# A two-layer hybrid attention backbone on one core: additions behind the value batches, neighbouring queries for the maxes, and a longer lead

## The chip, the cores and the metric

The kernel runs on one core of one Trainium2 chip. It is one program with one launch; its time is the device time of that launch in microseconds, and the median of several runs counts. The engines are named as the profile names them: PE (TensorE, matmuls), PEld (TensorE's weight loads, which run beside matmuls), DVE (VectorE), ACT (ScalarE), POOL (GpSimd) and SP (SyncE, which issues every DMA of this kernel, in program order).

## The reference

Two layers work on 2048 latent tokens and 256 context tokens of width 1024. In each layer the tokens are normalised and projected once; three mixers share the projection: an attention with low-rank queries and keys (six heads, here MLA), a grouped-query attention (six heads that share two key heads, here GQA), and a convolution. Their outputs are gated, concatenated and projected back. What the change touches is the softmax of the two attentions:

```python
def one_block(qi):
    s = jnp.einsum('bqgrd,bkgd->bgrqk', qi, k).astype(jnp.float32) * scale
    p = jax.nn.softmax(s, axis=-1).astype(v.dtype)
    return jnp.einsum('bgrqk,bkgv->bqgrv', p, v)
...
o_mla = block_attention(q_mla, jnp.concatenate([k_mla, k_mla_c], axis=1),
                        jnp.concatenate([v_mla, v_mla_c], axis=1))
...
y = jnp.concatenate([o_mla, o_gqa, o_conv], axis=-1) * jax.nn.silu(p[..., OFF_GATE:])
x_new = x + gate[:, None, :] * (y @ w_out)
```

All data are float32. Latent queries look at all 2304 keys. The first layer also computes the context tokens' own attention (256 queries, 256 keys); the last layer doesn't.

## The kernel before

The program alternates projections and attention: the projection of layer 0, the attention of layer 0, a stage that holds layer 0's output projection and layer 1's input projection, the attention of layer 1, and the last output projection. The change lies in `attention` (line 1369) and, in one place, in `first_unit` (line 1249), which belongs to the projections.

**Units and steps.** The attention of a layer runs through `units`: one for each head and each chunk of queries. The GQA heads (numbers 6 to 11) come first, then the MLA heads (0 to 5). A chunk has 512 queries; layer 0 has a fifth chunk with the 256 context queries. A unit has 9 steps (`j` from 0 to 8), each for a pair of 128-key tiles; the unit of the context chunk has one. The order of all the instructions is written out by the loop at line 1604: what one turn of it issues is one step.

**Scores.** `s_pair` (line 1478) issues the score matmuls of a step: two key tiles run side by side in the upper and lower 64 rows of the array, with 4 such pairs of matmuls for a GQA head and 5 for an MLA head. Values are split in a high and a low part, so there are several products. The last product (`qd`) adds the negated maximum of each query, which stands as a row of 512 numbers in partitions 32 and 96 of the tile `qd`. ACT then takes the exponential into a tile `p` of 128 x 1024, from a ring of 8 buffers (`buffer`, line 1388).

**Maxes.** The maximum of each query must be known before its unit starts. `max_stream` (line 1434) computes it ahead, from the high parts alone: for each of 4 groups of 128 queries it multiplies queries by keys into PSUM tiles `m` (three banks, `p_m`), and DVE reduces each bank to a column of `mx`. A generator turn issues one pair of banks of 512 keys (8 turns) or, in the ninth turn, all four groups with the last 128 keys, and then the final reduction into `nm`, 128 partitions x 4. Here the queries are the stationary operand: group q takes every fourth query, `x[r, q:512:4]`, so partition p of column q belongs to query 4p + q, and the four numbers of a partition are neighbours in the row. Each step of the loop takes one turn of this stream, and the first four steps two (`behind = LEAD - 9`), so that the stream stays `LEAD` = 13 turns ahead of the steps. The stream also loads the queries of the next unit when it starts a unit (`load_q`, line 1413; 4 DMAs for a GQA unit and 10 for an MLA unit, five sets of query buffers).

**Rows.** `rows_step` (line 1421) moves the maxes from `nm` to the row of `qd` through DRAM: one step after `nm` it issues the store, and two steps later the two loads into the partitions 32 and 96.

**Value batches.** `pv_pair` (line 1536) multiplies a tile `p` with the values into the PSUM tile `o`. These are not issued at once: the loop collects steps in `pend` and issues them as batches, 5 pairs at `j` = 5 and the last 4 at `j` = 0 of the next unit (line 1620; batches of 3 in the last head). With the last pair of a unit, ACT copies `o` to `e`, and two DMAs store it.

**Sums.** `sums` (line 1499) adds up the tiles `p` of a unit on POOL, one 128 x 1024 addition a step, into `acc`. In GQA units the last two tiles are first added on DVE (`d`), at `j` = 8, and POOL adds `d`. Three steps after the unit's last, at `j` = 2 of the next, `fold_step` (line 1524) adds the two halves of `acc` on DVE into `f`. `finish` (line 1557) sums `f` over the partitions with a matmul by ones, for two units at a time, at the head of a value batch.

**Beside it**, while the heads 0 to 5 run, a planner (`out_proj.sch.poll()`) mixes in tasks of the next output projection (`y_k`, line 622): they divide the attention's outputs by the sums and multiply with the gates, on DVE and ACT, in tiles `lent` and `big`.

Of the kernel before, what the change touches and what calls it, by code (L numbers as in the profile page):

```python
# [9 lines left out]
F32 = mybir.dt.float32  # L10
# [277 lines left out]
def hybrid_dit(ctx: ExitStack, tc: tile.TileContext, I: dict, out: bass.AP):  # L288
# [163 lines left out]
    def projections(l):  # L452
# [796 lines left out]
        def first_unit():  # L1249
# [16 lines left out]
            def lane():  # L1266
                while todo:
                    n, e, q = todo.pop(0)
                    o, w = n * 512, min(512, NK - n * 512)
                    ps = (yield from aux.take())[:, 0:w]  # L1270
                    r = slice(64 * e, 64 * e + 64)
                    T.matmul(out=ps, lhsT=a[r, q:512:4], rhs=kH[0][r, o:o + w], start=True, stop=True)
                    yield ps
                    V.tensor_reduce(out=mx[:, q, 2 * n + e:2 * n + e + 1], in_=ps, op=ALU.max, axis=AX.X)
                    aux.give(ps)
                    left[0] -= 1
                    yield
# [6 lines left out]
            row = z.nm[u]  # L1284
            save(row.rearrange("(p j) -> p j", p=128), nm, nt)
            yield lambda: INF if clk.pending[key(row)] else 0.0
# [82 lines left out]
    def attention(l, out_proj):  # L1369
        z = scratch[l]  # L1370
        with ExitStack() as ps_:
# [49 lines left out]
            def rows_step():  # L1421
                for r in rows_due:
                    r[0] -= 1
                    h, c = u = r[1]
                    row = z.nm[h, c]
                    if r[0] == ROW_OUT:
                        dma(row.rearrange("(p j) -> p j", p=128), r[2].bitcast(F32))
                    elif r[0] == 0:
                        for o, i in m_parts(u, qt[u], row):
                            dma(out=o, in_=i)  # L1430
                while rows_due and rows_due[0][0] <= 0:
                    rows_due.pop(0)

            def max_stream():
                for i, u in enumerate(units[1:], 1):
                    h, c = u
                    n = CH[c][1] // 128
                    if 1 < i + 1 < len(units):
                        load_q(units[i + 1])
                    a, _, cr, _ = qt[u]  # L1440
# [8 lines left out]
                    def scores(ps, q, o, w, at=0):  # L1449
                        for i, (x, y) in enumerate(ops):  # L1450
                            for e in range(2):
                                r = slice(64 * e, 64 * e + 64)
                                T.matmul(out=ps[e][:, at:at + w], lhsT=x[r, q:CH[c][1]:n], rhs=y[r, o:o + w],
                                         start=(i == 0), stop=(i == len(ops) - 1))
# [13 lines left out]
                    for e in range(2):  # L1468
# [3 lines left out]
                                    negate=True)  # L1472
                    rows_due.append([ROW_OUT + 1, u, nm[:, 0:n]])
                    yield
# [24 lines left out]
            def sums(u, j, p, N):  # L1499

                s = st.setdefault(u, {})
                side = u[0] >= MH and N > 2
                if j == 0:
                    s["acc"] = p
                    if N == 1:
                        folds.append([3, u])
                elif j == 1:
                    acc = ac.tile([128, 1024], F32, tag="acc", name="acc")
                    add(G, acc, s["acc"], p)
                    s["acc"] = acc  # L1510
                elif side and j == N - 2:
                    s["p"] = p
                elif side and j == N - 1:
                    d = buffer(u)
                    add(V, d, s.pop("p"), p)
                    add(G, s["acc"], s["acc"], d)
                else:
                    add(G, s["acc"], s["acc"], p)
                if j == N - 1 > 0:
                    folds.append([3, u])  # L1520

            folds = []

            def fold_step(now=False):

                for f in folds:
                    f[0] -= 1
                while folds and (now or folds[0][0] <= 0):
                    u = folds.pop(0)[1]
                    W = CH[u[1]][1]  # L1530
# [5 lines left out]
            def pv_pair(u, j, t, N, p):  # L1536
# [6 lines left out]
                for e in range(2):  # L1543
                    T.matmul(out=s["o"][e * 64:e * 64 + 64, :], lhsT=v[:, t + e, :], rhs=p[:, e * W:(e + 1) * W],
                             start=(j == 0), stop=(j == N - 1))
                if j == N - 1:
                    e1 = op.tile([128, 512], F32, tag="e1", name="e1")[:, 0:W]
                    A.activation(out=e1, in_=s["o"], func=AF.Copy)
# [5 lines left out]

            fin = []

# [23 lines left out]
            LAG = 1  # L1580
            ROW_OUT = 2
            LEAD = 13
            qt[units[0]], qt[units[1]] = qall[0:2]
# [20 lines left out]
            for u, j, t, N in steps:  # L1604
# [9 lines left out]
                if behind:  # L1614
                    behind -= 1
                    next(stream)
                fold_step()
                sums(u, j, p, N)
                pend.append((u, j, t, N, p))
                if len(pend) >= LAG + batch(pend):  # L1620
                    finish()
                    for x in [pend.pop(0) for _ in range(batch(pend))]:
                        pv_pair(*x)
                out_proj.sch.poll()
                h, c = u
# [3 lines left out]
            while pend:  # L1629
                finish()  # L1630
                for x in [pend.pop(0) for _ in range(batch(pend))]:
                    pv_pair(*x)
            fold_step(True)
            finish(True)
# [92 lines left out]
```

## Time and profile before

| what | value |
|---|---|
| median of 3 runs | 4333.98 us (4333.17 to 4342.68) |
| the profiled execution | 4335.15 us, of which 4333.4 us are its span |
| mean granted TensorE clock | 0.962 |
| attention of layer 0, GQA heads, then MLA heads | about 787 to 1386 us, then to 2075 us |
| attention of layer 1, GQA heads, then MLA heads | about 2930 to 3496 us, then to 4129 us |

The page of the profile gives each engine's busy time, and the share of the span that it is. The view of stretches gives the same for chosen stretches of time, with the clock that TensorE was granted (1.00 is full speed; it takes the values 1.0 and 0.5, so a mean of 0.93 says that 14% of the stretch ran at half speed). The view of waits tells for which engine's work an engine stood idle. In the rows of instructions a time in square brackets is the idle time of the engine just before, and what ended it. Nearly all instructions go through one helper and stand under one line, L159, so that the tiles tell them apart: `s` and `qd` are scores, `m` and `mx` maxes, `nm` the negated maxes, `f` the folds, `o` the value products, `e` their copies.

### The profile page before, as it was taken

Reading aid. Unit: us, or ns where it says so; the run is one execution under the profiler, and the core shown is the slowest. Engines: PE = TensorE matmul, PEld = TensorE weight load, DVE = VectorE, ACT = ScalarE, POOL = GpSimd, SP = SyncE. Lnnn points to the kernel's source line nnn. Section 1 sums busy time; section 2 is a strip of 40 time slices with the busy share of each in tenths; the row PEclk is TensorE's granted clock in tenths of the full one; section 3 lists DMA queues with packets and bytes.
Section 4 is the critical chain, followed back from the end, with each engine's and each line's share of the span. In section 5 each row is a group of like instructions: output and inputs, shape, how many; then the busy total and the mean of one; then the engine's idle time right before and its main releaser. Section 6 shows DMA issues by size and latency. Waiting matters only on the chain. (4 is left out here: it accounts for less than half of the span.)

```text
span 4333.4 us, 60999 instructions
## 1 busy us (share of the span) xinstructions
PE 4082.3 (94%) x22542; PEld 2834.6 (65%) x22542; DVE 2449.4 (57%) x3771; ACT 1891.8 (44%) x2503; POOL 2482.6 (57%) x1277
## 2 busy tenths in 40 slices
PE   7999899999999999999879998999999999999988
PEld 4778467665555666665668787776556566666566
DVE  4643378555655645456533554886555574555663
ACT  4553356444443333333334544664444444433342
POOL 2541263576766776666434423537777777777744
PEclk8999999999999999999989999999999999999999
DMA  5555454411313332233854453543121143232384
GB/s 184 158 163 166 155 163 156 93 39 36 60 39 71 96 74 56 66 67 103 244 184 154 139 174 122 172 145 68 35 57 38 43 103 69 66 77 62 102 260 146
DMA packets 384213, 477.13 MB, mean 110 GB/s; under 512 B 128190, under 2 KB 200583, under 8 KB 383915
## 3 DMA queue, kind: packets, MB, share of 16 engines
q1 hardware_dynamic: 383914, 473.24, 38.7%
q8 instruction: 177, 2.90, 0.3%
q14 instruction: 122, 0.99, 0.1%
HBM read 329.79 MB, written 134.85 MB: 107 GB/s over the span
## 5 line engine op out<-in xcount | busy, mean ns | idle before, releaser
L159 DVE TENSOR_REDUCE mx<-m 128x1 f32<-128x512 f32 (+2 forms) x1716 | 1084.5, 680 | 1020.8 <-PE m L159 1012.6
L159 PE MATMUL mm<-big,wh 128*128 128x512 f32 (+2 forms) x4240 | 1300.8, 390 | 74.0 <-DVE big L159 30.6
L159 POOL TENSOR_TENSOR acc<-acc,p 128x1024 f32<-128x1024 f32 x482 | 1183.6, 2456 | 279.6 <-ACT p L159 202.2
L159 ACT ACTIVATE p<-s 128x1024 f32<-128x1024 f32 (+1 forms) x682 | 695.2, 1020 | 874.7 <-PE s L159 789.1
L159 PEld LDWEIGHTS mm<-big,wh 128*128 128x128 f32 (+1 forms) x4240 | 776.1, 189 | 311.6 <-issue 77.2
L159 PE MATMUL s<-qh,big 64*128 64x512 f32 (+1 forms) x3504 | 829.9, 411 | 0.2
L159 PE MATMUL mm<-big,wl 128*128 128x512 f32 (+2 forms) x2120 | 808.7, 381 | 3.6 <-POOL wl L159 3.6
L159 POOL TENSOR_TENSOR wl<-wraw,wh 128x1024 fp32r<-128x1024 f32 (+2 forms) x148 | 314.4, 2130 | 740.7 <-ACT wh L159 688.1
L159 PE MATMUL o<-p,big 128*64 128x512 f32 (+1 forms) x2728 | 689.0, 622 | 0.7 <-ACT e L159 0.7
L159 PE MATMUL m<-big,qh 64*128 64x512 f32 (+1 forms) x2304 | 587.4, 412 | 96.8 <-DVE mx L159 96.6
L159 PEld LDWEIGHTS m<-big,qh 64*128 64x128 f32 x2304 | 491.6, 309 | 156.9 <-DVE mx L159 130.1
L159 PEld LDWEIGHTS s<-qh,big 64*128 64x128 f32 x3504 | 434.1, 189 | 197.3 <-issue 165.4
L159 PEld LDWEIGHTS mm<-big,wl 128*128 128x128 f32 (+1 forms) x2120 | 401.2, 189 | 83.3 <-POOL wl L159 4.9
L159 PEld LDWEIGHTS o<-p,big 128*64 128x64 f32 x2728 | 201.6, 144 | 377.8 <-issue 370.9
L159 PE MATMUL s<-ql,big 64*128 64x512 f32 (+1 forms) x1752 | 421.5, 393 | 0.0
L159 POOL TENSOR_TENSOR acc<-acc,wraw 128x1024 f32<-128x1024 f32 x142 | 344.4, 2426 | 81.8 <-ACT wraw L159 45.0
L159 DVE SCALAR_TENSOR_TENSOR aux<-wn,par,aux 128x512 f32<-128x512 f32 (+1 forms) x396 | 259.1, 720 | 121.8 <-ACT aux L159 121.4
L159 ACT ACTIVATE wraw<-s 128x1024 f32<-128x1024 f32 (+1 forms) x194 | 198.3, 1022 | 242.3 <-PE s L159 197.4
L159 POOL TENSOR_TENSOR sb<-sb,sb 128x512 f32<-128x512 f32 (+1 forms) x161 | 194.5, 1216 | 156.7 <-ACT sb L159 127.3
L159 PE MATMUL m<-big 64*128 64x512 f32 (+1 forms) x1032 | 261.8, 406 | 1.3 <-DMA big<-qm 1.2
L159 PE MATMUL s<-qd,zm 33*128 33x512 f32 (+1 forms) x876 | 234.7, 406 | 6.3 <-DMA qd<-nm 6.3
L159 POOL TENSOR_TENSOR acc<-p,p 128x1024 f32<-128x1024 f32 x52 | 124.8, 2399 | 199.4 <-ACT p L159 199.4
(168 smaller groups left out, 4772.1 us busy)
## 6 DMA issues: line engine op xcount, KB each, us to landing
wraw<-in_w_in SPq DMA_DIRECT2D x80, 512.0 KB
o<-e SPq DMA_DIRECT2D x192, 128.0 KB
big<-o SPq DMA_DIRECT2D x96, 256.0 KB
wraw<-in_w_out SPq DMA_DIRECT2D x48, 512.0 KB
sb<-in_w_mod SPq DMA_DIRECT2D x77, 256.0 KB
sb<-in_x SPq DMA_DIRECT2D x61, 256.0 KB
big<-kn SPq DMA_DIRECT2D x48, 288.0 KB
sb<-x SPq DMA_DIRECT2D x54, 256.0 KB
```

Source lines behind the costliest of these rows:

```text
L159: return f(**kw)
```

## The change

Five things change; the result computed is the same.

1. The fold and the DVE half of the sums move. The addition of the last two tiles `p` is issued by `pv_pair` with the unit's last value pair, behind the matmuls of that batch. The fold of a unit is issued behind the first batch after that whose head belongs to a unit of 9 steps. In the order of DVE's instructions the addition moves from `j` = 8 to `j` = 0 of the next unit, and the fold from `j` = 2 of the next unit to `j` = 5, in both cases behind the maxes of that step and with a value batch on PE.
2. A group of the maxes takes 128 neighbouring queries. Partition p of column q now belongs to query 128q + p, so the store of the row writes single numbers (512 pieces of 4 bytes instead of 128 of 16).
3. The two loads of a row come three steps after its store instead of two.
4. `LEAD` is 16 instead of 13: the first seven steps take two turns of the stream.
5. When the stream starts the fourth chunk of a head, it loads the queries of two units instead of one.

```diff
@@ first_unit
-                    T.matmul(out=ps, lhsT=a[r, q:512:4], rhs=kH[0][r, o:o + w], start=True, stop=True)
+                    T.matmul(out=ps, lhsT=a[r, q * 128:q * 128 + 128], rhs=kH[0][r, o:o + w], start=True, stop=True)
...
-            save(row.rearrange("(p j) -> p j", p=128), nm, nt)
+            save(row.rearrange("(j p) -> p j", p=128), nm, nt)
@@ rows_step
-                    if r[0] == ROW_OUT:
-                        dma(row.rearrange("(p j) -> p j", p=128), r[2].bitcast(F32))
+                    if r[0] == ROW_IN:
+                        dma(row.rearrange("(j p) -> p j", p=128), r[2].bitcast(F32))
                     elif r[0] == 0:
                         for o, i in m_parts(u, qt[u], row):
                             dma(out=o, in_=i)
...
+            loaded = [1]
+
             def max_stream():
                 for i, u in enumerate(units[1:], 1):
                     h, c = u
                     n = CH[c][1] // 128
-                    if 1 < i + 1 < len(units):
-                        load_q(units[i + 1])
+                    ahead = i + 2 if c == 3 else i + 1
+                    while loaded[0] < min(ahead, len(units) - 1):
+                        loaded[0] += 1
+                        load_q(units[loaded[0]])
...
-                                T.matmul(out=ps[e][:, at:at + w], lhsT=x[r, q:CH[c][1]:n], rhs=y[r, o:o + w],
+                                T.matmul(out=ps[e][:, at:at + w], lhsT=x[r, q * 128:q * 128 + 128], rhs=y[r, o:o + w],
...
-                    rows_due.append([ROW_OUT + 1, u, nm[:, 0:n]])
+                    rows_due.append([ROW_IN + 1, u, nm[:, 0:n]])
@@ sums
                 if j == 0:
                     s["acc"] = p
-                    if N == 1:
-                        folds.append([3, u])
...
                 elif side and j == N - 1:
-                    d = buffer(u)
-                    add(V, d, s.pop("p"), p)
-                    add(G, s["acc"], s["acc"], d)
+                    s["last"] = s.pop("p"), p, buffer(u)
                 else:
                     add(G, s["acc"], s["acc"], p)
-                if j == N - 1 > 0:
-                    folds.append([3, u])
...
-            def fold_step(now=False):
-
-                for f in folds:
-                    f[0] -= 1
-                while folds and (now or folds[0][0] <= 0):
-                    u = folds.pop(0)[1]
+            def fold_step():
+
+                while folds:
+                    u = folds.pop(0)
@@ pv_pair
                 if j == N - 1:
+                    if "last" in s:
+                        p0, p1, d = s.pop("last")
+                        add(V, d, p0, p1)
+                        add(G, s["acc"], s["acc"], d)
+                    ended.append(u)
@@ the loop
             LAG = 1
-            ROW_OUT = 2
-            LEAD = 13
+            ROW_IN = 3
+            LEAD = 16
...
-                fold_step()
                 sums(u, j, p, N)
                 pend.append((u, j, t, N, p))
                 if len(pend) >= LAG + batch(pend):
                     finish()
+                    if pend[0][3] > 1:
+                        folds += ended
+                        ended.clear()
                     for x in [pend.pop(0) for _ in range(batch(pend))]:
                         pv_pair(*x)
+                    fold_step()
...
-            fold_step(True)
+            folds += ended
+            fold_step()
             finish(True)
```

More of the change, by code (lines that the diff above doesn't have):

```diff
@@ L1553, in pv_pair @@
                     fin.append(u)
-            fin = []
+            fin, ended = [], []
             def finish(last=False):
```

## The prediction

> **What bounds the kernel now.** First the busy times of the page, then the view of stretches for the four parts of the two attentions (start and end, length, busy time of PE, PEld, DVE, ACT and POOL, granted clock):
>
> ```profile
> span 4333.4 us, 60999 instructions
> PE 4082.3 (94%) x22542; PEld 2834.6 (65%) x22542; DVE 2449.4 (57%) x3771; ACT 1891.8 (44%) x2503; POOL 2482.6 (57%) x1277
> ```
> ```profile
> 816.00:1360.00 544.00, 507.48 (x3050) 315.25 (x3052) 322.81 (x508) 228.43 (x247) 372.81 (x155) 0.93 0.20 44
> 1360.00:2070.00 710.00, 668.40 (x4466) 444.56 (x4464) 398.37 (x575) 269.37 (x297) 490.39 (x200) 0.98 0.33 77
> 2958.00:3472.00 514.00, 488.01 (x2960) 300.66 (x2958) 305.36 (x483) 222.72 (x232) 372.48 (x154) 0.94 0.18 42
> 3472.00:4122.00 650.00, 634.29 (x4306) 424.63 (x4306) 376.10 (x543) 261.10 (x277) 490.83 (x200) 0.99 0.33 80
> ```
>
> PE is the bound everywhere; a gain must come out of its idle time, its lost clock or its own work. In the GQA parts (first and third row) it idles 36.5 of 544 us and 26 of 514, and the clock is 0.93 and 0.94. The waits say for whom (total, times, longest): the rows `qd` in the whole run, then the maxes in the first and in the second GQA part.
>
> ```profile
> PE s L159 <- DMA qd<-nm: 22.7, 10, 3.4
> ```
> ```profile
> PE m L159 <- DVE mx L159: 32.7, 27, 2.2
> ```
> ```profile
> PE m L159 <- DVE mx L159: 23.4, 22, 1.1
> ```
>
> What DVE does at such a wait stands in the timeline of one GQA unit, DVE first, then PE:
>
> ```profile
> 962.02 1.50 DVE L159 TENSOR_TENSOR f<-acc 128x512 f32<-128x512 f32 x1
> 963.45 2.47 DVE L159 TENSOR_REDUCE mx<-m 128x1 f32<-128x512 f32 x4
> 966.34 1.29 DVE L159 TENSOR_REDUCE mx<-m 128x4 f32<-128x512 f32 x2 [0.42 <-PE m L159]
> 972.37 3.68 DVE L159 TENSOR_REDUCE mx<-m 128x1 f32<-128x512 f32 x6 [4.52 <-PE m L159]
> 975.96 1.22 DVE L159 TENSOR_TENSOR p<-p,wraw 128x1024 f32<-128x1024 f32 x1
> ```
> ```profile
> 962.76 0.39 PE L159 MATMUL m<-big,qh 64*128 64x512 f32 x1
> 964.18 0.62 PE L159 MATMUL m<-big,qh 64*128 64x512 f32 x1 [1.03 <-DVE mx L159]
> ```
>
> Two maxes a step take DVE about 1.2 us (four in 2.47), and a GQA step without a value batch is no longer than that. So the fold, 1.50 us between them, has no room: all three banks of `m` are full, and PE stands 1.03 us. Around the value batch the same DVE idles 4.52 us.
>
> The stall also costs clock. Four units of layer 1, two without and two with a lost window, then the 3.4 us that hold a stall and the 3.4 us behind them:
>
> ```profile
> 3240.00:3261.50 21.50, 20.42 (x134) 13.14 (x134) 13.93 (x23) 9.84 (x10) 16.99 (x7) 1.00 0.16 38
> 3331.10:3354.10 23.00, 21.93 (x134) 13.80 (x136) 13.86 (x21) 9.79 (x11) 16.93 (x7) 0.93 0.14 36
> 3308.70:3331.10 22.40, 21.33 (x138) 13.61 (x140) 13.92 (x23) 10.46 (x12) 16.97 (x7) 1.00 0.15 37
> 3354.10:3378.10 24.00, 22.93 (x138) 13.74 (x140) 13.97 (x23) 10.45 (x12) 16.92 (x7) 0.93 0.13 35
> ```
> ```profile
> 1013.40:1016.80 3.40, 2.34 (x20) 1.96 (x19) 2.98 (x4) 1.84 (x2) 3.32 (x2) 1.00 0.01 0
> 1016.80:1020.20 3.40, 3.40 (x13) 1.35 (x13) 2.27 (x5) 1.02 (x1) 3.24 (x3) 0.50 0.11 21
> ```
>
> Same work (x134 each, x138 each), 1.5 and 1.6 us longer at a mean of 0.93, which is 2 x 0.07 x 23 = 3.2 us at half clock. An us at half clock thus loses about 0.47 us.
>
> **The change part by part.** Everything is worked out against the profiled execution, 4335.15 us (span 4333.4); the median of the runs is 4333.98, 1.2 us less.
>
> *A, folds in the GQA parts.* Moved to `j` = 5, the fold starts after that step's maxes (DVE is through with those of 966.34 at 967.6) and has until the maxes of 972.37. The 4.5 us hold the 1.50 us, and also the two folds behind a context chunk (the longer one takes 2.65, below). The addition of 975.96 moves behind the maxes that follow it, into the same sort of gap at `j` = 0; POOL waits for it there as before, with a busy time of 17 us in a unit of 21.5. The stalls go: 32.7 + 23.4 = **56 us**. Late next is DVE itself, 2 x 0.6 us a step against PE's step, a few tenths in a unit, counted in E.
>
> *B, their clock.* 2 x 0.07 x 544 + 2 x 0.06 x 514 = 138 us at half clock, times 0.47: **65 us**. The rounding of the clock leaves 5 us either way.
>
> The page "TensorE: Matmul & The Clock Gate" of the Trainium skill (Part 1, The HAM clock gate) has the clock fall after a whole idle window of about 3.4 us. Here 1.06 us of idling (3.40 - 2.34) within a busy window was enough, so the trace doesn't bear it out; by the page B would be nothing, a rival below.
>
> *C, rows.* The loads of a row wait in SP's queue behind query loads: in the worst place, at the fourth chunk of an MLA head, ten DMAs of each of two units come between. A store and its loads in a GQA unit, and SP's waits for the landing of such a store:
>
> ```profile
> 3248.44 0.32 SPq L1366 DMA_DIRECT2D nm<-nm  x1
> ...
> 3251.29 0.68 SPq L1366 DMA_DIRECT2D qd<-nm  x2
> ```
> ```profile
> SPq L1366 <- DMA nm<-nm: 5.3, 5, 2.3
> ```
>
> Three more steps of lead, one of them spent before the loads, leave four steps instead of two between load and use: at least 2 x 1.2 = 2.4 us more, and at the fourth chunk ten of the twenty query loads are issued a unit earlier. The longest wait is 3.4 us. I take all of it, **23 us**. The MLA parts lose 2 x 0.02 x 710 + 2 x 0.01 x 650 = 41 us to half clock, 19 us by the same 0.47; of this I take half, **10 us**, for waits of this kind and of D, since other stalls stay.
> The store in 512 pieces isn't in the trace. From the issue of the store to its load 2.9 us pass now (3248.44, 3251.29), SP has waited for its landing 2.3 us at most. Between no change and four times that, 9 us, nothing comes late: seven steps and a value batch, some 13 us, lie between store and use. I take nothing.
>
> *D, folds behind the context chunk in MLA units of layer 0.* One of six such places, with both stalls, and the longer DVE fold of a GQA one:
>
> ```profile
> 1734.28 0.62 PE L159 MATMUL m<-big,qh 64*128 64x512 f32 x1 [1.32 <-DVE mx L159]
> ...
> 1736.80 0.45 PE L159 MATMUL m<-big,qh 64*128 64x128 f32 x1 [0.51 <-DVE mx L159]
> ```
> ```profile
> 984.27 2.65 DVE L159 TENSOR_TENSOR f<-acc 128x512 f32<-128x512 f32 x1
> ```
>
> 5 x 1.8, and 1.3 in the last head, which has the first stall alone: **10 us**. The stalls behind `lent` and `big` (the planner's tasks) stay.
>
> *E, neighbouring queries.* Weight loads of one form, strided in `m`, contiguous in `s`; then PE at the scores of a context unit, and from the start to the end of an MLA unit's ninth turn:
>
> ```profile
> L159 PEld LDWEIGHTS m<-big,qh 64*128 64x128 f32 x2304 | 491.6, 309 | 156.9 <-DVE mx L159 130.1 <-issue 0.4
> L159 PEld LDWEIGHTS s<-qh,big 64*128 64x128 f32 x3504 | 434.1, 189 | 197.3 <-issue 165.4 <-ACT p L159 3.2 <-ACT wh L159 0.8
> ```
> ```profile
> 974.54 0.28 PE L159 MATMUL s<-qh,big 64*128 64x256 f32 x1
> 974.66 0.28 PE L159 MATMUL s<-ql,big 64*128 64x256 f32 x1
> ```
> ```profile
> 3583.67 0.55 PE L159 MATMUL m<-big,qh 64*128 64x128 f32 x2
> ...
> 3585.47 0.45 PE L159 MATMUL s<-qh,big 64*128 64x512 f32 x1
> ```
>
> Under 512 columns the 309 ns are hidden by the matmul running. In the ninth turn the matmuls have 128 columns, and the load is the bound: 8 pairs in 1.80 us (3583.67 to 3585.47), 0.225 a pair. Contiguous loads kept up with 0.12 a pair (974.54, 974.66), so 8 x 0.105 = 0.84 us go in an MLA unit, 0.42 in a GQA unit, of which I take 0.3 because DVE's 1.2 us a step is late next. 48 x 0.84 + 46 x 0.3, and 3 us in the context units: **57 us**. Bounds: nothing, if the step of the queries isn't what makes the load long; 87 us, if a pair gets down to half of 0.12 us, as its columns are half of those at 974.54.
>
> The same page (section LDWEIGHTS) lets the time of a load hang on the number of columns alone. The 309 against 189 ns speak against that; by the page E would be nothing, the second rival.
>
> *F, the start of each attention.* Three more steps take two turns, and there DVE is the bound:
>
> ```profile
> 788.18 4.88 DVE L159 TENSOR_REDUCE mx<-m 128x1 f32<-128x512 f32 x8 [0.85 <-PE m L159]
> ```
>
> 2.44 us a step instead of 1.2: 3.7 us in a layer, with some half clock 4, so **8 us** more in two.
>
> ```profile
> 4107.87 19.35 POOL L159 TENSOR_TENSOR acc<-acc,p 128x1024 f32<-128x1024 f32 x7
> ```
>
> The steps at the end of an attention that have no maxes now gain nothing, since there POOL's additions, one behind the other to the end of the stage, set it.
>
> Sum: 56 + 65 + 23 + 10 + 10 + 57 - 8 = 213 us. 4334 - 213 = **4121 us**. The forecast's own range, from the rounding in B, half to all of C and D, and 35 to 75 us in E: 4080 to 4155.
>
> **The rivals.** *The clock stays*, because something else in each GQA unit halves it, such as the turn of 128-column matmuls: B and the 10 us are lost, 4121 + 75 = 4196 us. For it speaks that the lost window comes right behind that turn as well as behind the stall; against it, that MLA units with twice as long a turn run at 0.99. *The load stays long*, because of the operand and not its step: 4121 + 57 = 4178. Against it: the 2304 loads at 309 are all strided, the 3504 at 189 all contiguous. *The stall moves* on to `j` = 6 and 7, because the fold waits behind POOL in its new place for longer than the batch lasts: A and B are lost, 4121 + 121 = 4242. The 2.65 us of 984.27 are such a wait, and they fit in 4.52. *Slower*: the store of a row in 512 pieces takes so long that the scores wait for it at the first step of every unit. It decides from 13 us, 25 ns a piece if they go one by one; each us beyond costs 96 us in 96 units, so at 15.2 us everything is given back, and at 16 us it is 4121 + 288 = 4409. For it speaks only that no such store is in the trace; against it the 2.3 us that SP waited for one of 128 pieces.
>
> **How the numbers follow.** Forecast 0.66, load 0.10, clock 0.08, moved stall 0.06, slower 0.06; 0.04 is left for what I don't see, half of it within 0.2% of the time before, which is about what a measurement can tell from no change. Faster by more than 0.2%: 0.92; within: 0.02; slower: 0.06. The range holds the forecast's, the load's and the clock's cases: 4075 to 4197.
>
> **What would show it.** In the GQA parts the wait of `m` for `mx` near zero and the clock at 0.99 or more (A, B); folds under a value batch; no wait for `qd` (C); weight loads of `m` near 189 ns, the MLA turn near 1 us (E); more waits in the first unit (F). The forecast is wrong if GQA units without a stall still show windows at 0.5, if the loads of `m` stay at 309, or if SP stands at the store of the rows.

## The result, and the profile after

The changed kernel takes 4397.68 us (median of 4 runs, 4384.36 to 4405.24) against 4333.57 us before: 1.014 times the time, 95% interval 1.0108 to 1.0172. It is slower, by 64 us where 213 us less were forecast. The profiled execution took 4391.08 us. First the busy times of its page, then the view of stretches for the GQA and MLA parts of layer 0 and of layer 1:

```profile
span 4389.3 us, 61080 instructions
...
PE 4012.7 (91%) x22542; PEld 2670.0 (61%) x22542; DVE 2501.8 (57%) x3771; ACT 1892.2 (43%) x2504; POOL 2478.5 (56%) x1277
```
```profile
823.00:1345.00 522.00, 495.37 (x3214) 288.04 (x3216) 357.61 (x531) 238.15 (x257) 390.18 (x161) 0.97 0.33 48
1347.00:2071.00 724.00, 629.67 (x4281) 384.25 (x4282) 388.26 (x549) 259.23 (x287) 473.88 (x194) 0.92 0.37 74
2971.00:3476.00 505.00, 479.25 (x3126) 281.40 (x3126) 338.16 (x505) 232.58 (x242) 391.40 (x162) 0.97 0.28 45
3476.00:4177.00 701.00, 612.28 (x4134) 370.21 (x4133) 363.58 (x513) 250.07 (x265) 472.23 (x194) 0.92 0.34 71
```

The rows of the kernel before that the prediction shows hold other numbers of matmuls (3050 in the first, 3214 here). These stretches of the kernel before end with the same parts and hold about as many as the rows above:

```profile
814.00:1383.50 569.50, 532.66 (x3216) 331.34 (x3214) 337.43 (x533) 237.75 (x257) 391.78 (x162) 0.93 0.20 44
1384.00:2064.00 680.00, 639.45 (x4276) 426.47 (x4274) 378.58 (x550) 255.96 (x282) 467.58 (x191) 0.97 0.34 79
2951.00:3489.50 538.50, 512.16 (x3123) 317.14 (x3121) 320.07 (x508) 233.96 (x243) 390.68 (x162) 0.95 0.18 42
3490.00:4113.00 623.00, 607.65 (x4135) 407.92 (x4133) 358.59 (x524) 249.12 (x264) 468.20 (x191) 0.99 0.33 80
```

For about the same work the GQA parts (first and third row) became 48 and 34 us shorter, and their clock rose to 0.97. The MLA parts became 44 and 78 us longer: PE idles 94 of 724 us and 89 of 701 (41 of 680 and 15 of 623 before), and the clock fell from 0.97 and 0.99 to 0.92. The waits of the changed kernel say for what; first the maxes in the first GQA part, then the two rows that grew most, of PE and of SP's queue:

```profile
PE m L159 <- DVE mx L159: 0.4, 1, 0.4
```
```profile
PE s L159 <- DMA qd<-nm: 173.7, 47, 13.0
```
```profile
SPq L1366 <- DMA nm<-nm: 515.1, 95, 10.8
```

The stalls at the folds are gone (32.7 us before in the GQA part of layer 0). In their place PE waits 173.7 us for the rows of maxes, 22.7 before, and SP waits 515.1 us for the landing of the stores of such rows, 5.3 before. In the MLA parts PE also waits 60 us for the maxes, some 40 before. One of the waits for a row, in the view of the timeline, SP's queue first and then PE:

```profile
1604.76 0.38 SPq L1366 DMA_DIRECT2D nm<-nm  x1
1605.24 1.54 SPq L1366 DMA_DIRECT2D qh<-qm  x1
...
1609.51 0.59 SPq L1366 DMA_DIRECT2D ql<-qm  x1
1614.00 0.77 SPq L1366 DMA_DIRECT2D big<-qm  x2
...
1616.79 2.57 SPq L1366 DMA_DIRECT2D big<-kn  x4
1619.46 0.57 SPq L1366 DMA_DIRECT2D big<-vm  x1
1620.08 5.27 SPq L1366 DMA_DIRECT2D qd<-nm  x2
```
```profile
1627.89 1.04 PE L159 MATMUL s<-qd,big 33*128 33x512 f32 x2 [5.98 <-DMA qd<-nm]
```

The store of a row is issued at 1604.76. Seven loads of queries follow. The eighth transfer behind the store is issued only at 1614.00, the moment the store has landed: the transfers of this program mark their landings on eight semaphores in turn, and the one that this load needs is the store's own. The two loads of the row come last, at 1620.08, behind the rest of the queries and five loads of keys and values, and PE stands for 5.98 us.

When a transfer has landed can be read from the landing marks in the trace. Here are the medians in us from the issue, for the rows of 512 queries stored in the GQA heads of layer 0 (24 in each kernel) and for the 56 loads `qh` of queries in the same stretch, in all the kernels of this study that bear on it:

```
kernel                       the row's store                     lands after     loads qh<-qg after
before                       128 pieces of 16 bytes              1.4             3.5
changed                      512 pieces of 4 bytes               9.5             9.5
e1, turned rows              128 pieces of 128 bytes             1.4             2.6
e3, store beside             512 of 4 bytes, dense               9.5             9.4
e7, the same from ScalarE    512 of 4 bytes, dense               9.7             9.6
e11, half of it              256 of 4 bytes, dense               9.1             9.0
e12, spaced                  512 of 4 bytes, 64 bytes apart      2.1             2.8
```

The prediction had bounded the store at 9 us from issue to load and concluded that nothing comes late by that. The bound was nearly right. What it left out stands in the last column: what is issued behind the store lands late too.

### The profile page after: what moved, and what is told of

It reads as the page before. It is cut to its first block, busy times and chain, and to the rows that moved or that the text cites. A ratio compares the mean times of both kernels' runs of the same rounds, so it can differ in the third digit from the quotient of the medians.

```text
span 4389.3 us, 61080 instructions
## 1 busy us (share of the span) xinstructions
PE 4012.7 (91%) x22542; PEld 2670.0 (61%) x22542; DVE 2501.8 (57%) x3771; ACT 1892.2 (43%) x2504; POOL 2478.5 (56%) x1277
## 4 chain that ended last, share of the span: by engine, by line
PE 74%; DMA 15%; DVE 5%; SPq 2%; issue 2%; POOL 1%; ACT 1%; POOLq 0%; DVEq 0%; ACTq 0%
PE mm L159 29%; PE s L159 18%; PE o L159 15%; PE m L159 7%; PE aux L159 6%; DMA nm<-nm 4%; DMA qd<-nm 4%; SPq L1366 2%; DVE lent L159 2%; DVE mx L159 2%; DMA lent<-rc 1%; DVE big L159 1%; DMA ql<-qg 1%; DMA ql<-qm 1%; SPq L244 1%
## 5 line engine op out<-in xcount | busy, mean ns | idle before, releaser
L159 PE MATMUL mm<-big,wh 128*128 128x512 f32 (+2 forms) x4240 | 1304.7, 391 | 73.1 <-DVE big L159 29.9
L159 PE MATMUL s<-qh,big 64*128 64x512 f32 (+1 forms) x3504 | 794.6, 413 | 3.8 <-ACT p L159 3.6
L159 PE MATMUL m<-big,qh 64*128 64x512 f32 (+1 forms) x2304 | 473.9, 367 | 67.7 <-DVE mx L159 66.5
L159 PEld LDWEIGHTS s<-qh,big 64*128 64x128 f32 x3504 | 390.8, 188 | 218.3 <-issue 165.4
L159 PE MATMUL s<-ql,big 64*128 64x512 f32 (+1 forms) x1752 | 388.9, 394 | 0.0
L159 PEld LDWEIGHTS m<-big,qh 64*128 64x128 f32 x2304 | 294.6, 192 | 148.0 <-DVE mx L159 112.9
L159 PE MATMUL s<-qd,big 33*128 33x512 f32 (+1 forms) x876 | 195.5, 414 | 114.5 <-DMA qd<-nm 114.5
L159 PE MATMUL s<-qd,zm 33*128 33x512 f32 (+1 forms) x876 | 216.6, 407 | 59.4 <-DMA qd<-nm 59.3
```

What stands on the lines that cost most here:

```text
L159: return f(**kw)
```

## The experiments

The ratios are to the kernel before, with their 95% intervals.

**e1, rows turned.** If the pieces are the harm, other pieces must take it away. VectorE turns the maxes in blocks of 32 x 32, so that 32 neighbouring numbers lie in one partition; the whole tile is stored in 128 pieces, and the loads pick the four lines of each block.

```diff
-                    nm = mp.tile([128, 4], F32R, tag="nm", name="nm")
+                    nm = mp.tile([128, 32], F32, tag="nm", name="nm")
...
-                    V.tensor_reduce(out=nm[:, 0:n], in_=mx[:, 0:n, 0 if c < 4 else 4:6], op=ALU.max, axis=AX.X,
+                    V.tensor_reduce(out=nmt[:, 0:n], in_=mx[:, 0:n, 0 if c < 4 else 4:6], op=ALU.max, axis=AX.X,
                                     negate=True)
+                    V.transpose(out=nm, in_=nmt.bitcast(F32))
@@ rows_step
-                        dma(row.rearrange("(j p) -> p j", p=128), r[2].bitcast(F32))
+                        dma(row.rearrange("(p x) -> p x", p=128), r[2])
```

> The changed kernel, but a row of maxes is turned by VectorE (one 32x32-block transpose) and stored in 128 pieces of 128 bytes, not in 512 of 4 bytes; its loads read 16 pieces of 128 bytes. Theory P (the pieces): the store of 512 pieces lands only 9.5 us after its issue; that keeps the row's own loads back and, because the eighth DMA behind it waits for it, SP's whole queue. Then here SP waits for the landing of such stores under 40 us (515 in the changed kernel), PE waits for qd under 30 us (174), and the time is 4100 to 4180 us. Rival L (the loads): the earlier query loads, up to twenty DMAs at the fourth chunk, stand ahead of the row's loads whatever the store takes: waits for qd stay above 100 us and the time above 4300.

Measured: 4171.96 us, 0.9628 times the time before (0.9608 to 0.9647). The row's store lands after 1.4 us. The waits and the stretches of this kernel:

```profile
PE s L159 <- DMA qd<-nt: 29.9, 13, 7.2
```
```profile
SPq L1367 <- DMA nt<-nm: 27.3, 15, 3.7
```
```profile
823.00:1314.00 491.00, 482.52 (x3210) 284.53 (x3210) 356.14 (x560) 237.69 (x256) 391.06 (x162) 0.99 0.22 52
1317.00:1956.00 639.00, 603.25 (x4280) 374.44 (x4276) 399.40 (x576) 258.16 (x285) 478.50 (x194) 0.98 0.35 85
2857.00:3341.00 484.00, 475.00 (x3124) 280.37 (x3124) 336.40 (x528) 232.51 (x241) 390.81 (x162) 0.99 0.20 48
3341.00:3963.00 622.00, 591.25 (x4137) 364.98 (x4136) 383.91 (x535) 250.38 (x265) 475.43 (x194) 0.97 0.33 81
```

Theory P holds. The store of the rows in 512 pieces costs the changed kernel 4397.68 - 4171.96 = 226 us. An estimate puts most of it down to two things: 173.7 - 29.9 = 144 us of PE waiting for rows, and the clock, whose mean over the span is 0.946 in the changed kernel and 0.966 here. That is 2 x 0.054 x 4389 - 2 x 0.034 x 4175 = 190 us more at half clock, times the 0.47 of the prediction 89 us; together 233, where the two profiled executions, from which these figures come, differ by 214.

**e2, strided queries again.** The changed kernel without its neighbouring queries, in `first_unit` and in `attention`:

```diff
-                                T.matmul(out=ps[e][:, at:at + w], lhsT=x[r, q * 128:q * 128 + 128], rhs=y[r, o:o + w],
+                                T.matmul(out=ps[e][:, at:at + w], lhsT=x[r, q:CH[c][1]:n], rhs=y[r, o:o + w],
...
-                        dma(row.rearrange("(j p) -> p j", p=128), r[2].bitcast(F32))
+                        dma(row.rearrange("(p j) -> p j", p=128), r[2].bitcast(F32))
```

> The changed kernel without its neighbouring queries: maxes take every fourth query again, rows are stored in 128 pieces of 16 bytes. Theory P: waits for qd under 30 us, weight loads of m back at about 309 ns, and a time about 57 us above the kernel with turned rows (the price of the strided loads by the prediction), 4150 to 4240. Rival L: waits for qd above 100 us and a time above 4350.

Measured: 4201.98 us, 0.9697 (0.9669 to 0.9724), and PE waits 30.1 us for `qd`. The weight loads of this kernel, then two neighbouring units of the GQA heads and two of the MLA heads; then the same rows of e1:

```profile
L159 PEld LDWEIGHTS m<-big,qh 64*128 64x128 f32 x2304 | 450.2, 308 | 82.9 <-DVE mx L159 53.6
```
```profile
3123.98:3144.27 20.29, 20.29 (x134) 13.14 (x136) 14.29 (x23) 9.83 (x11) 15.90 (x7) 1.00 0.25 67
3144.27:3165.41 21.14, 21.14 (x138) 13.39 (x140) 14.25 (x21) 10.43 (x12) 17.87 (x8) 1.00 0.06 14
3604.03:3628.43 24.40, 24.40 (x176) 16.87 (x178) 14.39 (x22) 9.83 (x11) 19.37 (x8) 1.00 0.34 88
3628.43:3653.69 25.26, 25.26 (x180) 16.95 (x182) 14.21 (x20) 10.43 (x12) 19.39 (x8) 1.00 0.05 12
```
```profile
L159 PEld LDWEIGHTS m<-big,qh 64*128 64x128 f32 x2304 | 295.1, 191 | 147.8 <-DVE mx L159 108.9 <-ACT sb L159 1.8
```
```profile
3109.87:3129.77 19.90, 19.83 (x134) 11.99 (x136) 14.71 (x24) 9.83 (x10) 15.75 (x7) 1.00 0.26 69
3129.77:3150.50 20.73, 20.70 (x138) 12.09 (x138) 14.56 (x22) 10.43 (x11) 17.83 (x8) 1.00 0.07 15
3593.02:3616.49 23.47, 23.47 (x176) 14.76 (x176) 12.67 (x23) 9.84 (x10) 19.64 (x8) 1.00 0.35 92
3616.49:3640.86 24.37, 24.37 (x180) 15.65 (x180) 14.71 (x21) 10.44 (x11) 19.41 (x8) 1.00 0.06 13
```

Read the lengths of units with the same number of matmuls, all without a stall. Neighbouring queries save 0.4 us in a GQA unit and 0.9 in an MLA unit, and the load falls from 308 to 191 ns. The step of the queries makes the load long. By these rows 48 x 0.9 + 46 x 0.4 = 62 us go in the units; the whole kernel gains only 30. Of the rest 19 us are given back in the first unit of each attention: from its first score to the next unit's it takes 32.0 and 37.4 us in e1, 24.7 and 25.7 in e2. In layer 1 the reason is its row, which is made in the projection and still stored in 512 pieces in e1 (e10 below); for layer 0 that isn't shown, since the changed kernel has the same store and takes 24.1 us there. The remaining 13 us are not explained.

**e4, neighbouring queries alone.** The kernel before with part 2 of the change and nothing else: the diff of e2, read the other way round.

> The kernel before with one part of the change alone: neighbouring queries, so rows stored in 512 pieces, with the old lead (two steps from the store to the loads, two from there to the use). Theory P: the store's 9.5 us are longer than the two steps, so PE waits for qd at nearly every unit, over 200 us in all, and the time is 4400 to 4600. Rival L: without the earlier query loads the pieces do little, and the time is 4334 less the 57 us of the faster weight loads, 4260 to 4300.

Measured: 4753.83 us, 1.0976 (1.0944 to 1.1007), above what Theory P gave. The wait of this kernel:

```profile
PE s L159 <- DMA qd<-nm: 291.6, 85, 9.5
```

With the old lead nearly every unit waits, 85 times, and 118 us longer in all than in the changed kernel. So the longer lead did hide a good part of the slow store there. (The folds of e4 are in their old places too, so the whole difference of the two kernels, 356 us, isn't the lead's.)

**e3, e7, e11, e12: what is it about the store?** All four are the kernel of e1 with a second store beside the row's own, which nobody reads. In e3 SP issues it, in e7 ScalarE; in e11 it has half the pieces; in e12 each piece goes to an address 64 bytes from the next.

```diff
                         dma(row.rearrange("(p x) -> p x", p=128), r[2])
+                        dma(z.nm[h, c].rearrange("(j p) -> p j", p=128), r[2][:, 0:CH[c][1] // 128])   # e3
+                        nc.scalar.dma_start(out=z.nm[h, c].rearrange("(j p) -> p j", p=128), in_=r[2][:, 0:CH[c][1] // 128])   # e7
+                        dma(z.nm[h, c][0:CH[c][1] // 2].rearrange("(j p) -> p j", p=128), r[2][:, 0:CH[c][1] // 256])   # e11
+                        dma(z.ns[h, c].rearrange("(j p x) -> p j x", p=128, x=16)[:, :, 0], r[2][:, 0:CH[c][1] // 128])   # e12
```

> The kernel with turned rows, and beside each row's store a second one of 512 pieces of 4 bytes that nobody reads. It parts two ways in which the slow store can do harm. If the queue is what suffers (the eighth DMA behind it waits for its landing, and other transfers queue behind its pieces), SP's waits for nm stay above 300 us, PE waits for qd above 80 us and the time is above 4280. If only the row's own loads suffer, which wait for their store, the time is within 20 us of the kernel with turned rows.

> As the kernel with a second store of 512 pieces beside the turned rows, but this second store is issued by ScalarE and not by SP. If the harm of the slow store lies in SP's queue (the eighth DMA behind it waits for its landing), the waits for qd go back below 50 us and the time below 4230. If it lies in the transfer engines, which take 512 pieces whoever issued them, the waits stay above 150 us and the time above 4350.

> As the kernel with a second store of 512 pieces beside the turned rows, but with 256 pieces. That store should land after about 5 us instead of 9.7. If each piece costs the same, half of the 317 us come back: 4330 us. If there is a point from which it hurts, as the queue has slack until then, it is much less: 4180 to 4240 us.

> As the kernel with a second store of 512 pieces of 4 bytes beside the turned rows, but each piece goes to an address of its own 64 bytes from the next, not into one dense stretch. If the store is slow because its pieces fall into the same short stretches of memory, whose writes follow one another, it now lands in under 3 us and the time is 4170 to 4230 us. If each small piece costs by itself, it lands after 9 to 10 us as before and the time stays at 4440 to 4500.

Measured: e3 4489.30 us, 1.0357 (1.0332 to 1.0382); e7 4474.42, 1.032 (1.0301 to 1.034); e11 4437.63, 1.0232 (1.0205 to 1.0259); e12 4184.92, 0.9658 (0.9638 to 0.9677). PE's wait for the rows in e3, e7, e11 and e12:

```profile
PE s L159 <- DMA qd<-nt: 220.3, 66, 13.2
```
```profile
PE s L159 <- DMA qd<-nt: 190.3, 53, 12.0
```
```profile
PE s L159 <- DMA qd<-nt: 187.6, 52, 12.6
```
```profile
PE s L159 <- DMA qd<-nt: 29.8, 10, 7.9
```

e3: a store that nobody reads does even more harm than the real one, 317 us over e1 (SP's waits for it, 296 us, stay just under the 300 expected). So it isn't only that the row's loads wait for their store; everything behind it is late. e7: it doesn't help to issue it elsewhere. This does not quite part SP's queue from the transfer engines, as was meant, because the eight semaphores are shared by both issuers and SP still waits:

```profile
SPq L1367 <- DMA nm<-nm: 331.7, 63, 7.5
```

But loads that SP issues right behind such a store, without any wait, land late as well (9.4 to 9.6 us in the table instead of 2.6), and in the changed kernel the store at 1604.76 and the seven loads behind it all land between 1613.9 and 1617.6. The last two figures of a stretch, the busy share of the transfer engines and the GB/s that they moved, say the same, here while that store is outstanding and after it has landed:

```profile
1607.50:1614.00 6.50, 6.50 (x48) 3.89 (x46) 5.08 (x8) 3.08 (x3) 6.34 (x3) 1.00 0.37 66
1615.50:1617.50 2.00, 2.00 (x18) 1.35 (x16) 1.69 (x1) 0.09 (x1) 1.41 (x1) 1.00 0.55 191
```

The seven loads are issued by 1610, but until 1614 they move at a third of the later rate. In e7 the row's own quick store is hit too: of 30 such stores in the GQA heads of layer 0, which land after 1.4 us in e1, 16 land only after 8 to 11 us, though SP issues them and ScalarE the slow one. So the transfer engines are held up, whoever issues; the eighth transfer's wait comes on top, and how much of the time is its share stays open.

e11: half of the pieces cost nearly as much, 266 of 317 us, and land after 9.1 us. The expectation, either half or much less, was wrong both ways. e12: the same 512 pieces, spread out, land after 2.1 us, and the 13 us over e1 are within the noise, as the two intervals overlap.

The rows of the context chunks (256 queries, six of them in the GQA heads of layer 0) settle more. Their stores land after 9.6 us in the changed kernel (256 dense pieces of 4 bytes), after 9.4 in e11 (128 of 4 bytes), after 3.5 in the kernel before (128 of 8 bytes), and after 1.6 in e12 (256 of 4 bytes, spaced). So from 128 to 512 dense pieces of 4 bytes the time stays between 9 and 10 us, and with 128 dense pieces it falls from 9.4 to 3.5 to 1.4 us as a piece grows from 4 to 8 to 16 bytes. It is neither the number of pieces nor, by e12, their 4 bytes, but that they lie densely: 16, 8 and 4 such pieces share each 64 bytes of memory, in e12 one. That writes into one short stretch follow one another, while different stretches are written side by side, is the reading that fits them all; the traces don't show the memory itself, and no other spacing than 64 bytes was tried.

The page "DMA: Bandwidth & Descriptors" of the Trainium skill (Specifications) has transfers below 512 bytes do a read-modify-write, and its section "Issuing engines are not separate DMA queues" puts the transfers of all issuers on the same 16 engines. The second agrees with e7, where loads that SP issues land after 9.6 us beside a store that ScalarE issues. The first would bear the slow store out, but it names the size alone, and by the size alone e12 would be slow too; its 2.1 us say that density decides.

**e13, small pieces on the reading side.** Rows are stored as before, in 16-byte pieces, and the loads of the changed kernel put them in order.

```diff
-                        dma(row.rearrange("(j p) -> p j", p=128), r[2].bitcast(F32))
+                        dma(row.rearrange("(p j) -> p j", p=128), r[2].bitcast(F32))
                     elif r[0] == 0:
-                        for o, i in m_parts(u, qt[u], row):
-                            dma(out=o, in_=i)
+                        W = CH[c][1]
+                        i = row.rearrange("(p j) -> j p", p=128).unsqueeze(0)
+                        for e in (32, 96):
+                            dma(out=qt[u][3][e:e + 1, 0:W].bitcast(F32).rearrange("e (j p) -> e j p", p=128), in_=i)
```

> The changed kernel, but a row is stored as before in 128 pieces of 16 bytes, and its two loads put it into the order of neighbouring queries, reading 512 pieces of 4 bytes each. If only small writes into neighbouring addresses of the memory outside are slow, the waits for qd stay under 40 us and the time is 4160 to 4200 us. If small pieces are slow as such, 1024 of them a unit cost at least what 512 did: above 4390 us.

Measured: 4258.60 us, 0.9821 (0.9804 to 0.9837), between the two times expected. PE waits 91.2 us for `qd` in 41 places. A load of 512 pieces of 4 bytes lands after 4.9 us, the one of e1 after 1.9. Small pieces cost on the reading side too, 87 us over e1 where the dense writes cost 226, and nothing queues behind them for long (`qh` lands after 3.5 us, as in the kernel before; 2.6 in e1).

**e9, the folds and additions alone.** The kernel before with part 1 of the change and nothing else: the parts `sums`, `fold_step` and `pv_pair` of the diff, and of the loop

```diff
-                fold_step()
                 sums(u, j, p, N)
...
                     finish()
+                    if pend[0][3] > 1:
+                        folds += ended
+                        ended.clear()
                     for x in [pend.pop(0) for _ in range(batch(pend))]:
                         pv_pair(*x)
+                    fold_step()
```

> The kernel before with one part of the change alone: VectorE's additions and folds at the value batches. By the prediction's terms (stalls 56, their clock 65, MLA units 10): 4334 - 131 = 4203 us, with waits of m for mx near 40 us or less (96.6 before) and a clock of 0.99 in the GQA parts. Rival: the clock does not hang on that stall; then only the stalls go: 4334 - 66 = 4268 us with the clock of the GQA parts still at 0.93.

Measured: 4208.13 us, 0.9706 (0.9684 to 0.9727), 127 us less than before where 131 were expected. Its stretches, GQA parts first and third, and the wait of the maxes in the whole run:

```profile
815.00:1331.00 516.00, 500.50 (x3206) 318.82 (x3204) 352.23 (x531) 237.80 (x256) 391.41 (x162) 0.98 0.22 49
...
2883.00:3365.00 482.00, 477.41 (x3116) 309.13 (x3112) 333.03 (x505) 232.65 (x241) 390.79 (x162) 0.99 0.20 47
```
```profile
PE m L159 <- DVE mx L159: 28.4, 18, 3.3
```

The clock did hang on the stall: 0.98 and 0.99 where it was 0.93 and 0.94.

**e6, old folds in the kernel of e1.** The other way round: parts 2 to 5 with turned rows, and the old places of part 1, the diff of e9 read the other way round.

> The kernel with turned rows, and VectorE's additions and folds in their old places. The prediction priced their move at 56 us of stalls, 65 us of clock and 10 us in the MLA units: 4172 + 131 = 4303 us, with waits of m for mx near 100 us and a granted clock of 0.93 to 0.95 in the GQA parts. Rival: with neighbouring queries and more lead VectorE has room, or the clock does not hang on that stall, and only the stalls come back: 4172 + 56 = 4228 or less.

Measured: 4296.96 us, 0.9905 (0.9881 to 0.9929), 125 us over e1. The sum is the expected one, but it lies elsewhere. The GQA parts, one GQA unit, and one MLA unit:

```profile
824.00:1355.00 531.00, 499.78 (x3214) 293.27 (x3214) 330.33 (x560) 237.76 (x257) 390.34 (x162) 0.96 0.21 48
2926.00:3430.00 504.00, 480.95 (x3124) 280.74 (x3122) 310.60 (x528) 232.55 (x241) 390.60 (x162) 0.99 0.20 46
3053.10:3073.80 20.70, 20.06 (x134) 11.81 (x134) 13.40 (x22) 9.83 (x10) 16.87 (x8) 1.00 0.16 40
1504.70:1532.00 27.30, 25.57 (x176) 15.53 (x178) 14.80 (x24) 9.88 (x11) 19.35 (x8) 0.94 0.24 62
```

The GQA parts are 531 - 491 = 40 and 504 - 484 = 20 us longer than in e1, half of what the prediction had for them: in layer 1 the stall is 0.64 us now (20.70 - 20.06), and that doesn't halve the clock. More than that is lost in the MLA units, most of which stall some 1.7 us at the fold (27.30 - 25.57 = 1.73 in the last row), as they did not before. So the stall isn't a fixed price of the fold; it is the fold against the step that it falls in, and parts 2 and 4 moved that.

**e8 and e5, the lead.** Both are the kernel of e1. e8 has the old lead; e5 leaves the lead and moves the loads of the next head's keys and values:

```diff
@@ e8
-                    ahead = i + 2 if c == 3 else i + 1
+                    ahead = i + 1
...
-            ROW_IN = 3
-            LEAD = 16
+            ROW_IN = 2
+            LEAD = 13
@@ e5
-                if c == 0 and j == LAG + 1 and (h < MH or (h - MH) % 3 == 0):
+                if c == 0 and j == LAG + 5 and (h < MH or (h - MH) % 3 == 0):
```

> The kernel with turned rows and the old lead: LEAD 13, two steps from the store to the loads, each unit's queries loaded one unit ahead at every chunk. The prediction gave the longer lead 23 us of waits and up to 10 us of clock, less 8 us at the starts: 4172 + 25 = 4197 us. The traces so far let me expect less: the waits for qd are 29.9 us with the longer lead and were 22.7 before, and each attention's first unit ends 7 us later. So 4150 to 4175, with waits for qd at the fourth chunks again.

> The kernel with turned rows, and the loads of the next head's keys and values four steps later (at j = 6 of the head's first chunk instead of j = 2). In the kernel with turned rows PE still waits 29.9 us for qd in 13 places, one in nearly each head, and there the row's loads stand right behind five loads of keys and values of 288 to 576 KB. Theory K (those loads are in the way): the waits fall below 10 us, and the time by 30 to 50 us, to 4120 to 4145. Rival: the row is late because of the ten or twenty query loads; then the waits stay at 20 us or more and the time within 15 us of 4172.

Measured: e8 4185.46 us, 0.9656 (0.9632 to 0.968), just above its range, with 38.7 us of waits for `qd` from `nt`, 29.9 in e1; e5 4133.75, 0.9541 (0.9516 to 0.9566), with 7.0 us in two rows, of which the first is that of the first units (4.7 in e1):

```profile
PE s L159 <- DMA qd<-nm: 4.6, 2, 3.6
...
PE s L159 <- DMA qd<-nt: 2.4, 3, 1.5
```

e8 is 13.5 us over e1, but the two intervals overlap; e2 against e9, the same lead with strided queries, gives 6 us, also within the noise. So the longer lead by itself is worth little. It didn't take the waits away, it carried them from the fourth chunk of a head to the first: there the row's loads now stand right behind five loads of keys and values. In e1:

```profile
1449.54 2.58 SPq L1367 DMA_DIRECT2D big<-kn  x4
1452.20 0.57 SPq L1367 DMA_DIRECT2D big<-vm  x1
1452.83 4.95 SPq L1367 DMA_DIRECT2D qd<-nt  x2
```

Four steps later these big loads are in nobody's way, and 38 us go.

**e10, the best version.** e5, and the row of each layer's first unit is turned too.

```diff
             V.tensor_reduce(out=nm, in_=mx, op=ALU.max, axis=AX.X, negate=True)
+            V.transpose(out=mt[:, 32:64], in_=nt[:, 0:32].bitcast(F32))
...
-            save(row.rearrange("(j p) -> p j", p=128), nm, nt)
+            save(row.rearrange("(p x) -> p x", p=128), mt[:, 32:64], mt)
```

> The kernel with turned rows and late loads of keys and values, and the row of each layer's first unit, which is made in the projection, turned and stored in 128 pieces too. The first unit of layer 1 takes 42.6 us in that kernel and 30.9 in the one with strided queries, whose store has 128 pieces. If that store is the reason: 5 to 12 us less in layer 1, less than 8 in layer 0, 4113 to 4128 us. If the doubled steps at the start are: 4134 as before.

Measured: 4123.19 us, 0.9512 (0.9491 to 0.9534). It has the lowest median of all. The interval overlaps with that of e5, but in the traces the first unit of layer 1, from its first score to its last value product, takes 30.2 us instead of 42.6. The GQA parts run at full clock with next to no idle time of PE, first and second layer:

```profile
815.00:1300.00 485.00, 482.19 (x3212) 285.73 (x3210) 354.85 (x560) 237.61 (x256) 391.67 (x162) 1.00 0.22 53
...
2815.00:3290.00 475.00, 471.64 (x3124) 279.19 (x3122) 336.30 (x528) 232.97 (x241) 390.98 (x162) 1.00 0.20 49
```

## Why the prediction was wrong

**The step that failed** is the one in C on the store: "Between no change and four times that, 9 us, nothing comes late: seven steps and a value batch, some 13 us, lie between store and use. I take nothing." The size was nearly right (9.5 us), the conclusion wrong. It followed the row alone, from its store to its use. It didn't ask what else SP issues meanwhile: up to twenty loads of queries and five of keys and values, which land behind the store, hold SP at the eighth, and stand ahead of the row's own loads. The price is 226 us (e1), and some 12 more for the store of the same kind in the first unit of layer 1 (e10).

**The rival "slower"** had the right mechanism and the wrong point. It was to decide from 13 us, 25 ns a piece; the harm is there at 9.5 us, and not at the first step of every unit but at 47 places. It counted by pieces, and e11 and e12 show that the number of pieces isn't what counts. That its 4409 us lie near the 4398 measured is luck: they belong to 16 us a store and a wait of 3 us in each of 96 units.

**A, B and D**, folds, their clock, MLA units: 131 us forecast, 127 measured by themselves (e9). One reading behind B was too simple: the two units that the prediction shows at full clock idle 1.08 and 1.07 us, as much as the two with a lost window, so the stall doesn't cost clock each time. As a mean over the part the term held. In the changed kernel the waits of the maxes in the GQA parts are near zero, as said; the clock there is 0.97, not 0.99, because of the waits for rows, and 0.99 without them (e1).

**C**, 23 us of waits and 10 of clock: wrong also without the slow store. The waits remained (29.9 us in e1, and 4.7 at the first units, against 22.7 before), behind other loads; the longer lead gave 6 to 13.5 us, F included, within the noise, where 25 were counted. What was late next was not asked for here either.

**E**, neighbouring queries: mechanism right (191 ns in place of 308). In unstalled units the gain is 0.4 and 0.9 us, near the 0.3 and 0.84 taken; of 57 us the whole kernel shows 30, 19 of the rest lost again at the first units (e2).

**F**, the starts: 8 us taken. The first unit of layer 0 takes 24.1 us as before, that of layer 1 37.4 instead of 21.2. Of these 16 us more, 12 are that unit's own slow store (e10), which no step had.

**The range** of 4080 to 4155 doesn't quite follow from its terms: 5 us either way in B, half of C and D, and 35 to 75 us in E give about 4098 to 4170, or 4088 if all of the 19 us of clock in C are counted. The measured time lies far outside either.

Put together: 4334 before, 4208 with the folds moved (e9), 4202 with the lead too (e2), 4172 with neighbouring queries and a quick store (e1), 4398 with the slow one. That e10 ends at 4123, two us from the forecast, does not bear the forecast out: it needs three repairs that the forecast did not have.

## What to carry to other kernels

Price a transfer not by its own path alone but by what is issued behind it: a store that nobody reads cost 317 us here. Where a layout turns neighbouring numbers into a store of single numbers, turn them on an engine first, or give each its own stretch of memory (64 bytes in e12); dense 4-byte writes are the thing to avoid. And when a lead is lengthened, look which transfers now stand ahead of the one that was late: moving the big loads gave 38 us, more than the lead did.

## What the runs showed of the hardware that was not expected

- Dense writes of 4 bytes land 9 to 10 us after their issue, whether 512 of them go into 2 KB (9.5), 256 into 1 KB (9.1 in e11) or 128 into 512 bytes (9.4 in e11); 128 of 8 bytes land after 3.5, 128 of 16 bytes after 1.4, and 512 of 4 bytes that lie 64 bytes apart after 2.1.
- While such writes are under way, the loads behind them are held up with them (`qh` 9.5 us instead of 2.6), whichever engine issued the store.
- The length of a stall alone doesn't say whether the clock falls. Of 36 GQA units of the kernel before whose one stall of PE was 1.0 to 1.1 us long, 27 lost a window of 3.4 us or more at half clock and 9 did not. In e6 none of 37 GQA units with one stall of 0.5 to 0.95 us did, and neither did an MLA unit with one of 1.72 us (at 1734 us).
